# Input projection of the second and third token group by seven block products for eight (RetNet and HGRN2 decoder layer, one core)

## The chip, the cores and the metric

The kernel runs on one core of a Trainium2 chip. The metric is device time in microseconds of one execution, the median of several; lower is better. TensorE (PE) multiplies 128x128 weight blocks with up to 512 columns of activations into PSUM; VectorE (DVE), ScalarE (ACT) and GpSimd (POOL) do everything elementwise; SyncE (SP) issues the DMAs.

## The reference, cut to what matters

One decoder layer over 2048 prompt tokens and 8 sample sequences of 8 tokens (64 tokens, each sequence with a state of its own):

```
h    = rmsnorm(x) ; proj = h @ w_in                  # 1024 -> 4096: eight parts of 4 heads x 128
rq, rk, rv, rg, hq, hf, hi, hg = split(proj)
retention(rotary(rq), rotary(rk), rv), head norm, * silu(rg)         # 4 heads
f = lb + (1 - lb) * sigmoid(hf) ; HGRN2(silu(hq), 1 - f, hi, f), head norm, * silu(hg)   # 4 heads
x   += concat(o_r, o_h) @ w_out
x   += relu(rmsnorm(x) @ w_up)**2 @ w_down           # 1024 -> 4096 -> 1024
y    = rmsnorm(x) ; also the final states of both recurrences
```

## The kernel before

**Data.** Activations lie transposed, 128 features in the partitions and tokens in the columns. Every fp32 operand is cut into two parts, `hi` (rounded to the format `F32R`) and `lo` (the rest), and a product is three matmuls: hi·hi, hi·lo, lo·hi. A weight comes from DRAM as `raw`, 128x1024, 512 KB; ACT makes `hi` (line 270), DVE makes `lo` (line 284).

**Groups.** The 2112 tokens go through in three groups (`GROUPS`): 640 prompt tokens; 768 prompt tokens; the 64 sample tokens with 640 prompt tokens (704). First all three groups are mixed, one after the other (input projection, both recurrences, output projection: about 0 to 361, 361 to 781 and 781 to 1188 us), then all three go through the feed-forward layers (1188 us to the end).

**Input projection.** `proj` (line 341) makes one column block of 128 outputs: 8 row blocks x 3 products x 2 column pieces of half a group, 48 matmuls. Each head p needs six such blocks (parts 5 = f, 4 = q, 0 and 1 = rotary q and k, 7 and 3 = the two gates) and two weights for the values (`values`, line 748, 256 columns each). PSUM tiles `pj` of two banks take turns, two in all. The input is not normalised before the product: DVE multiplies the result by the factor `rs` of each token (`normed`, line 649; the values on ACT, line 758; the rotary tables on POOL, line 594). So `norm_in` of the next group (x loaded once, cut, squares added) only has to end before the first result is read.

**Order of work.** The program is written out by hand in *ticks*: every second wide matmul calls `tick`, which issues what `at` or `later` has put down for that tick. `mixer` puts the two recurrences of one head on this agenda: six levels of decays (`exponents` on POOL, lines 894 and 895; `decays` on ACT; `decayed` on DVE, lines 905 and 906), then states, outputs and gates; it needs 174 ticks in a group of 768, while a head's projection gives 192. `side` holds a second list in ticks: `plan_sums` makes the weight sums of the feed-forward layers (line 1243) beside the mixing of groups two and three.

**Weights kept.** In the first group `next_weight` (line 318) writes `hi` and `lo` of 32 of the 40 mixing weights to DRAM; the later groups read both parts back (line 253) instead of cutting them anew. The feed-forward layers already use the seven-product scheme (`product`, line 1211, `PRODUCTS`, `OCTET`): 24 matmuls of half a group each.

**Buffers.** 44 slabs of 128x768 (`sl`), 6 load tiles (`ld`), 3 + 4 tiles `raw`/`sum`, 3 + 3 tiles `hi`/`lo`.

Of the kernel before, what the change touches and what calls it, by code (L numbers as in the profile page):

```python
# [15 lines left out]
P = 128  # L16
D = 1024
KB = D // P
# [11 lines left out]
NSLAB = 44  # L30
NLD = 6
# [9 lines left out]
GROUPS = ((0, 0, 640), (0, 640, 768), (NS, 1408, 640))  # L41
# [35 lines left out]
              ("A12", "B21", True, ((0, 0),)))  # L77

# [68 lines left out]
def in_blocks():  # L147
    for p in range(H):
        if p:
            yield from ((7, p - 1), (3, p - 1))  # L150
        yield from ((5, p), (4, p), (0, p), (1, p), ("v", p))
    yield from ((7, H - 1), (3, H - 1))

# [46 lines left out]
class Kernel:  # L200
# [43 lines left out]
    def weight(self, i):  # L244
        n = len(self.stream)
        while self.w_next < min(i + 1 + self.ahead, n):
            j = self.w_next
            e = self.stream[j]
            if e[0] == "p":
# [7 lines left out]
            while self.w_load <= j or j >= W_UQ0 and self.w_load <= j + 2 and self.w_load < n:  # L257
                if self.stream[self.w_load][0] == "p":
                    break
                k, later = self.w_load, self.w_load >= self.n_sums  # L260
                other = later and k % 7 % 2
                raw = self.raws[k] = self.wp.tile([P, WT], F32, tag="sum" if other else "raw", name="raw",
                                                  bufs=4 if other else 3)
# [22 lines left out]
    def plan_stream(self):  # L286
# [6 lines left out]
        def mixing():  # L293
            self.stream += [("p" if N_MADE <= j < N_KEPT else "w", j) for j in range(W_UQ0)]
# [8 lines left out]
        mixing()  # L303
        mixing()
# [5 lines left out]

    def next_weight(self):
# [3 lines left out]
        if N_MADE <= i < N_KEPT:  # L315
# [61 lines left out]
    def build(self):  # L377
        nc, tc, I = self.nc, self.tc, self.I
        with ExitStack() as ctx:
# [15 lines left out]
            self.wts, self.second, self.kept = {}, {}, {}  # L395
# [25 lines left out]
            for ns, p0, n in GROUPS:  # L421
# [6 lines left out]
                g.segs = [list(range(first)), list(range(first, nch))]  # L428
                gs.append(g)
            nc.scalar.dma_start(vec, I["vec"])  # L430
            nc.scalar.preload_act_table_set("natural_log_exp_and_others")
            self.norm_in(gs[0], True)
# [10 lines left out]
            self.hs = cp.tile([P, KB * P], F32R, name="hs")  # L443
# [9 lines left out]
            at = [16] + [141 + 192 * (j // 2) + 85 * (j % 2) for j in range(2 * H - 1)]  # L453
            self.plan_sums(sums[:NQ], at)
            self.mix(gs[1])
            self.out_proj(gs[1], 1, lambda: self.norm_in(gs[2], pace=12))
# [78 lines left out]
    def norm_in(self, g, start=False, pace=5):  # L535
# [6 lines left out]
        def piece(kb):  # L542
            x, hi, lo = self.x_block(g, kb, start), self.getr(), self.getr()
            if start and kb == 0:
                self.ahead = 0
                self.weight(0)
# [3 lines left out]
                                           op0=ALU.mult, op1=ALU.subtract)  # L550
            if g.ns:
# [3 lines left out]
            g.h.append((hi, lo))  # L555
            if start:
                g.x.append(x)
            else:
                g.sq = self.add_square(g, g.sq, x, nc.vector)
# [52 lines left out]
        else:  # L612
            for kb in range(KB):
                self.later(pace * kb, piece, kb)
        t0 = 66 if start else pace * KB
        self.later(0 if start else t0, tables)
        if not start:
            self.later(t0 + 9, split)
        self.later(t0 + (0 if start else 20), factor)
        self.later(t0 + 24, rotary)  # L620
        self.later(t0 + 24, factor_t)

    def mix(self, g):
        nc = self.nc
        if g.ns:
            g.qm = [self.get(), self.get()]
            for q in g.qm:
                nc.gpsimd.memset(q, 0.0)
# [3 lines left out]
        for p in range(H):  # L632
            b = {}
            if prev is not None:
                self.gates(g, prev)
            self.project(g, p, b)
            end = self.mixer(g, p, b, max(self.now, end))
# [1190 lines left out]
```

## Time and profile before

| | us |
|---|---|
| median of 3 runs | 2493.01 (2492.97 to 2494.5) |
| profiled execution, first to last instruction (its span) | 2490.7 |
| median beyond that span | 2.3 |
| PE busy / DVE / ACT / POOL in the profiled execution | 2478.4 / 1868.8 / 1246.4 / 377.3 |
| bytes moved by DMA | 525.44 MB, mean 211 GB/s |

The page gives no other time for the profiled execution than its span; what lies around it is taken as the 2.3 us to the median. A busy PE is not always a PE at its best rate, since matmuls overlap in the pipeline; so rates are read from runs of matmuls without a gap, as time by count.

### The profile page before, as it was taken

To read this page: it belongs to the slowest core of one execution; us is meant where nothing else is said; L and a number is where in the kernel's file an instruction comes from. 1 tells how busy PE (TensorE), PEld (TensorE's weight loads), DVE (VectorE), ACT (ScalarE), POOL (GpSimd) and SP (SyncE) were. 2 spreads that over 40 slices of the span, in tenths; PEclk is the share of its full clock that TensorE was granted. 3 is DMA by queue.
4 is the path that set the end of the run, shared out by engine and by line. 5 is a ranking of instruction groups with operands and counts; after the bars stand their busy time and mean duration, and the time that the engine had idled before them with its cause. 6 is when DMAs were issued, how large, how long until landed. Compare 5 with 4: busy or idle time off the path is not lost.

```text
span 2490.7 us, 41430 instructions
## 1 busy us (share of the span) xinstructions
PE 2478.4 (100%) x16520; PEld 2461.9 (99%) x16520; DVE 1868.8 (75%) x2453; ACT 1246.4 (50%) x1674; POOL 377.3 (15%) x320
## 2 busy tenths in 40 slices
PE   9999999999999999999999999999999999999998
PEld 9999999999999999999999999999999999999998
DVE  7666766667685666686775899776699878778987
ACT  6665663444464444453644545444454436445544
POOL 5223304324421442340000000000000000000000
PEclk9999999999999999999999999999999999999999
DMA  7454575465566665768876866576675545867552
GB/s 265 166 185 170 203 259 178 161 229 186 184 210 236 220 219 200 266 211 270 283 213 221 280 198 213 174 239 222 203 262 177 188 151 190 288 196 247 194 189 89
DMA packets 191655, 525.44 MB, mean 211 GB/s; under 512 B 20963, under 2 KB 62563, under 8 KB 191462
## 3 DMA queue, kind: packets, MB, share of 16 engines
q1 hardware_dynamic: 191318, 522.77, 62.3%
q8 instruction: 130, 2.13, 0.4%
q14 instruction: 63, 0.52, 0.1%
q10 hardware_dynamic: 144, 0.02, 0.0%
HBM read 389.28 MB, written 132.39 MB: 209 GB/s over the span
## 4 chain that ended last, share of the span: by engine, by line
PE 98%; DVE 1%; DMA 0%; ACT 0%; issue 0%; SPq 0%; DVEq 0%
PE pj L341 29%; PE pf L1211 26%; PE pj L1211 25%; PE pjv L748 8%; PE mm L920 2%; PE mm L1108 1%; PE po L1100 1%; PE po L1102 1%; PE mm L977 1%; PE mm L512 1%; PE mm L511 1%; PE po L784 1%; PE mm L1034 1%; PE mm L850 1%; DMA lo<-w33lo 0%; DMA slab<-x 0%
## 5 line engine op out<-in xcount | busy, mean ns | idle before, releaser
L270 ACT CAST hi<-raw 128x1024 fp32r<-128x1024 f32 x392 | 411.8, 1050 | 616.6 <-PE pf L1211 258.4
L341 PE MATMUL pj<-slab,hi 128*128 128x320 f32 (+2 forms) x3072 | 661.4, 328 | 1.8 <-DVE slab L649 1.0
L1211 PE MATMUL pf<-slab,hi 128*128 128x320 f32 (+2 forms) x2768 | 657.6, 321 | 0.0
L1211 PE MATMUL pj<-slab,hi 128*128 128x352 f32 (+2 forms) x2608 | 620.6, 322 | 0.0
L284 DVE TENSOR_TENSOR lo<-raw,hi 128x1024 fp32r<-128x1024 f32 x392 | 485.6, 1239 | 113.6 <-ACT hi L270 108.1
L341 PEld LDWEIGHTS pj<-slab,hi 128*128 128x128 f32 x3072 | 508.3, 188 | 3.9 <-DVE slab L649 1.2
L1211 PEld LDWEIGHTS pf<-slab,hi 128*128 128x128 f32 x2768 | 480.1, 188 | 0.0
L1211 PEld LDWEIGHTS pj<-slab,hi 128*128 128x128 f32 x2608 | 452.9, 188 | 0.1
L1211 PE MATMUL pf<-slab,lo 128*128 128x320 f32 (+2 forms) x1384 | 444.1, 321 | 0.0
L1211 PE MATMUL pj<-slab,lo 128*128 128x352 f32 (+2 forms) x1304 | 419.1, 321 | 0.0
L341 PE MATMUL pj<-slab,lo 128*128 128x320 f32 (+2 forms) x1536 | 379.5, 327 | 0.5 <-DVE lo L284 0.4
L341 PEld LDWEIGHTS pj<-slab,lo 128*128 128x128 f32 x1536 | 263.6, 188 | 1.6 <-DVE lo L284 1.0
L1211 PEld LDWEIGHTS pf<-slab,lo 128*128 128x128 f32 x1384 | 259.6, 188 | 0.0
L1211 PEld LDWEIGHTS pj<-slab,lo 128*128 128x128 f32 x1304 | 244.6, 188 | 0.0
L748 PE MATMUL pjv<-hi,slab 128*128 128x256 f32 x1024 | 193.3, 285 | 0.0
L1302 ACT CAST slab<-slab 128x640 fp32r<-128x640 f32 (+2 forms) x192 | 145.2, 778 | 64.0 <-DVE slab L1313 51.7
L1306 DVE TENSOR_TENSOR slab<-slab 128x640 fp32r<-128x640 f32 (+2 forms) x192 | 167.0, 884 | 8.5 <-PE pj L1211 2.8
L748 PEld LDWEIGHTS pjv<-hi,slab 128*128 128x128 f32 x1024 | 162.2, 192 | 1.4
L748 PE MATMUL pjv<-lo,slab 128*128 128x256 f32 x512 | 144.8, 283 | 0.0
L899 ACT ACTIVATE slab<-slab 128x640 f32<-128x640 f32 (+2 forms) x72 | 56.3, 782 | 147.7 <-POOL slab L895 147.4
L1556 DVE TENSOR_TENSOR slab<-pf,slab 128x640 f32<-128x640 f32 (+2 forms) x88 | 77.5, 886 | 29.4 <-PE pf L1211 28.9
L748 PEld LDWEIGHTS pjv<-lo,slab 128*128 128x128 f32 x512 | 98.1, 192 | 0.0
(222 smaller groups left out, 3009.0 us busy)
## 6 DMA issues: line engine op xcount, KB each, us to landing
raw<-w SPq DMA_DIRECT2D x264, 512.0 KB, 4.3
slab<-u SPq DMA_DIRECT2D x32, 384.0 KB, 4.8
u<-ld SPq DMA_DIRECT2D x30, 384.0 KB, 4.0
slab<-u SPq DMA_DIRECT2D x32, 352.0 KB, 5.0
u<-ld SPq DMA_DIRECT2D x30, 352.0 KB, 3.9
slab<-u SPq DMA_DIRECT2D x32, 320.0 KB, 4.6
u<-ld SPq DMA_DIRECT2D x30, 320.0 KB, 4.3
ld<-x SPq DMA_DIRECT2D x16, 384.0 KB, 3.8
```

Source lines behind the costliest of these rows:

```text
L270: self.nc.scalar.copy(hi, raw)
L284: self.nc.vector.tensor_tensor(out=lo, in0=self.second.pop(j), in1=hi.bitcast(F32), op=ALU.subtract)
L341: self.nc.tensor.matmul(pj[:, i, :T2], w, a[:, c0:c1], start=j == 0 and q == 0, stop=j == n - 1 and q == 2)
L511: self.nc.tensor.matmul(ps, self.ones_r, hi, start=True, stop=False)
L512: self.nc.tensor.matmul(ps, self.ones_r, lo, start=False, stop=True)
L748: nc.tensor.matmul(pj[:, i * 256:(i + 1) * 256], a[:, s:s + C], ww, start=kb == 0 and q == 0, stop=kb == KB - 1 and q == 2)
L899: nc.scalar.activation(x["dd", w][:, a:T], x["dd", w][:, a:T], AF.Exp)
L920: nc.tensor.matmul(ps[:, j], qk[:, cols[c]], second(qk[:, cols[c]]), start=True, stop=True)
L1211: self.nc.tensor.matmul(*a, **k)
L1302: self.nc.scalar.copy(hi[:, :g.T], B[name][:, :g.T])
L1306: self.nc.vector.tensor_tensor(out=lo[:, :g.T], in0=B[name][:, :g.T], in1=hi.bitcast(F32)[:, :g.T], op=ALU.subtract)
L1556: nc.vector.tensor_tensor(out=r, in0=ps, in1=r, op=ALU.add)
```

## The change

- **Groups** become 64 sample + 512 prompt tokens (576), 768 and 768: the sample moves into the first group.
- **Pairs of blocks.** In groups two and three the blocks of one head are taken in pairs, (5, 4), (0, 1) and (7, 3). A pair is a 2x2 arrangement of blocks of the weights (row halves by the two columns of the pair) times the 2x2 blocks of the activations (row halves by token halves). `quad` forms it by seven products in place of eight: 7 x 4 x 3 = 84 matmuls of 384 columns in place of 96. Ten pairs of each group go this way; the first head's (5, 4) and (0, 1), and all values, stay as they were.
- **Weight sums.** `plan_quads` makes S1 to S4 of each pair in the first group, on the side list, one pair every 80 ticks: four half loads (256 KB), four sums of 128x512 on POOL, four casts on ACT, four `lo` parts on DVE, eight stores of 256 KB. The other three operands are stored from the weights of group one (`next_weight`). A *unit* of 512 KB holds `hi` and `lo` of one product's weights; groups two and three read seven units for each pair, up to six ahead.
- **Activation sums.** Sums need normalised input, so `norm_in` of groups two and three reads x, adds squares, forms the factor, reads x again, scales and cuts it; `plan_sides` reads x a third time and makes T1 to T4.
- **Elementwise work.** The results need no factor any more (no `normed`, no scaled tables). In all groups `1 - f` enters as a logarithm (`lk`), so that one of the two products of `decayed` goes; several slabs are reused in place.
- **Order in groups two and three.** The last head's gates come before its values; heads are stored to DRAM (`put_heads`) and read back (`get_heads`).
- **Buffers.** 49 slabs, 5 load tiles, 4 `raw` and no `sum`.

```
-GROUPS = ((0, 0, 640), (0, 640, 768), (NS, 1408, 640))
+GROUPS = ((NS, 0, 512), (0, 512, 768), (0, 1280, 768))
+QUAD = (("A11", "B11"), ("S2", "T2"), ("S3", "T3"), ("S1", "T1"), ("A12", "B21"), ("A22", "T4"), ("S4", "B22"))
...
+    def plan_quads(self, start, each):
...
+        def make(x, name, a, op, b, into):
+            order(nc.gpsimd.tensor_tensor(out=x[into], in0=x[a], in1=x[b], op=op))
...
+        def second(x, name):
+            order(nc.vector.tensor_tensor(out=x[name].bitcast(F32R), in0=x[name], in1=x["hi", name].bitcast(F32), op=ALU.subtract))
+        def keep(x, key, name):
+            unit = self.unit(key + (name,))
+            order(nc.sync.dma_start(unit[:, :n], x.pop(("hi", name)).bitcast(F32)))
+            order(nc.sync.dma_start(unit[:, n:], x.pop(name)))
...
+            self.plan_quads(110, 80)
             self.mix(gs[0])
-            self.out_proj(gs[0], 1, lambda: self.norm_in(gs[1], pace=12))
+            self.out_proj(gs[0], 1, lambda: self.norm_in(gs[1], pace=6))
...
+        def scaled(kb):
+            x, hi, lo = self.x_block(g, kb), self.getr(), self.getr()
+            nc.vector.scalar_tensor_tensor(out=x[:, :T], in0=x[:, :T], scalar=self.vec[:, V_MIX + kb:V_MIX + kb + 1],
+                                           in1=g.rs[:, :T], op0=ALU.mult, op1=ALU.mult)
+            nc.scalar.copy(hi[:, :T], x[:, :T])
...
+    def quad(self, g):
...
+        for k, (A, B) in enumerate(QUAD):
+            if k in (0, 2):
+                t = self.pj.tile([P, 2, 512], F32, tag="pj", name="pj")
+                x[k], x[k + 1] = t[:, 0, :T2], t[:, 1, :T2]
+            ps, first = x[(0, 1, 2, 3, 0, 2, 3)[k]], k < 4
+            wh, wl = self.next_weight()
...
+                for q, (w, a) in enumerate(((wh, ah), (wh, al), (wl, ah))):
+                    nc.tensor.matmul(ps, w[:, c], a, start=first and kb == q == 0, stop=kb == KB // 2 - 1 and q == 2,
+                                     skip_group_check=not first)
...
+            if k == 0:
+                nc.scalar.copy(s[:, one], ps)
+            elif k == 1:
+                add(s[:, one], ps, s[:, one])
+            elif k == 2:
+                nc.scalar.copy(s[:, two], ps)
+            elif k == 3:
+                add(s[:, two], ps, s[:, two])
+                nc.gpsimd.tensor_tensor(out=Q[:, two], in0=s[:, two], in1=s[:, one], op=ALU.add)
+            elif k == 4:
+                nc.scalar.copy(F[:, one], ps)
+            elif k == 5:
+                add(Q[:, one], ps, s[:, one])
+            else:
+                add(F[:, two], ps, s[:, one])
...
-            nc.vector.tensor_tensor(out=Q4[:, :, 0, :], in0=D4[:, :, 0, :], in1=blocks(k, w, a)[:, :, 0, :], op=ALU.mult)
...
-        at(t + 12, tt, nc.vector, _Lazy(x, "kd"), _Lazy(x, "kd"), k)
```

More of the change, by code (lines that the diff above doesn't have):

```diff
@@ L152, in in_blocks, with in_places, in_quads @@
     yield from ((7, H - 1), (3, H - 1))
+def in_places():
+    out, i = {}, 0
+    for part, p in in_blocks():
+        out[part, p] = i
+        i += 2 if part == "v" else 1
+    return out
+def in_quads():
+    for p in range(H):
+        if p:
+            yield from ((5, 4, p), (0, 1, p))
+        yield 7, 3, p
 def lay_out_weights(w_in, w_out, w_up, w_down):
@@ L611, in norm_in @@
             self.at(24 + 2 * KB, both)
[L612 to L621, printed above, removed]
+            self.later(0, tables)
+            self.later(66, factor)
+            self.later(90, rotary)
+            self.later(90, factor_t)
+            return
+        for kb in range(KB):
+            self.later(pace * kb, squares, kb)
+        t0 = pace * KB
+        self.later(t0 + 4, split)
+        self.later(t0 + 12, factor)
+        g.h = [None] * KB
+        for k in range(KB):
+            self.later(t0 + 20 + 9 * k, scaled, k)
+        self.later(t0 + 92, tables)
     def mix(self, g):
@@ L1178, in mixer @@
             t += 4
+        if g.scaled and p < H - 1:
+            at(t + 22, self.put_heads, g, p)
         if p == H - 1:
```

333 lines of the change are left out of this document (262 added, 71 removed).

## The prediction

> **What bounds the kernel now.** I read the page's busy times first, then the busy times by stage, then who held PE, then the chain of waits for PE's rate in each stage.
>
> ```profile
> PE 2478.4 (100%) x16520; PEld 2461.9 (99%) x16520; DVE 1868.8 (75%) x2453; ACT 1246.4 (50%) x1674; POOL 377.3 (15%) x320
> ```
> ```profile
> 0.00:361.00 361.00, 358.70 (x2665) 353.43 (x2666) 258.75 (x418) 229.03 (x340) 113.71 (x100) 1.00 0.57 202
> 361.00:781.00 420.00, 420.00 (x2864) 415.44 (x2863) 286.53 (x414) 195.99 (x287) 137.87 (x104) 1.00 0.56 199
> 781.00:1188.00 407.00, 406.01 (x2904) 400.76 (x2903) 273.80 (x462) 183.12 (x295) 125.69 (x116) 1.00 0.69 236
> 1188.00:2490.00 1302.00, 1293.68 (x8093) 1292.24 (x8091) 1049.70 (x1160) 638.30 (x756) 0.00 (x0) 1.00 0.64 210
> ```
> ```profile
> PE pj L341 <- DVE slab L649: 1.0, 1, 1.0
> PE pj L341 <- DVE slab L1271: 0.8, 1, 0.8
> PE pj L341 <- DVE lo L284: 0.4, 1, 0.4
> ```
> Columns of the second fence: length, then busy PE, weight loads, DVE, ACT, POOL, granted clock, DMA share, GB/s. PE has no gap in any stage: its longest waits for data in the projections are a microsecond and less. The clock is 1.00, so there is nothing to win there. The kernel ends when PE has issued its matmuls. Fewer matmuls shorten it one for one, until another resource is late.
>
> What a matmul costs, from gapless runs in the chain of waits (start, length, count):
> ```profile
> 394.31 14.03 PE pjv L748 x117
> 478.24 4.18 PE pj L341 x24
> 1399.91 7.04 PE pf L1211 x48
> 1607.94 8.32 PE pj L1211 x48
> 2265.77 7.63 PE pf L1211 x48
> ```
> Columns 256, 384, 320, 384, 352 take 119.9, 174.2, 146.7, 173.3 and 159.0 ns. From 320 to 384 columns that is 0.417 ns a column with 13.3 ns on top, and 256 columns lie on the same line (120.0). So the column count sets the rate, though every matmul loads its own weights:
> ```profile
> L341 PEld LDWEIGHTS pj<-slab,hi 128*128 128x128 f32 x3072 | 508.3, 188 | 3.9 <-DVE slab L649 1.2 <-DVE slab L1271 1.0 <-DVE slab L549 0.2
> L341 PE MATMUL pj<-slab,hi 128*128 128x320 f32 (+2 forms) x3072 | 661.4, 328 | 1.8 <-DVE slab L649 1.0 <-DVE slab L1271 0.8
> ```
> Loads equal matmuls: the two column pieces of a block share no load today. Working on one token half at a time therefore loses nothing.
>
> **The change part by part.**
>
> *Matmuls.* A pair of blocks falls from 96 to 84 matmuls of 384 columns. Ten pairs in each of two groups: 20 x 12 = 240, at 174.2 ns = 41.8 us, all of it on the path. The Trainium skill, "TensorE: Matmul & The Clock Gate", section "Back-to-back issue gap", gives N/2.4 + 2.5 ns, 162.5 ns for 384; by that the saving would be 39.0 us. The trace has 174.2 and decides.
>
> *New group sizes.* A group has 24 x 48 + 8 x 48 = 1536 projection matmuls and 16 x 7 x 24 = 2688 in the feed-forward layers. 640 to 576 takes 32 columns off each (4224 x 13.3 ns = 56.3 us), 704 to 768 adds 173.3 − 159.0 = 14.4 ns (60.7 us). On the straight line the two cancel, by the rows they add 4.4: I take 2, the middle. Chunks and sample are only exchanged between groups.
>
> *PE's floor:* 2490.7 − 41.8 + 2 = 2450.9 in the profile; with the 2.3 us by which the median exceeds the span, 2453.2. All else has to be hidden under PE; group one is the place to look, as it loses about 18 us of cover (361 less 1536 x 13.3 ns = 20.5, plus some 3 for the sample: 343) and gains the weight sums and the sample.
>
> *DVE, group one.*
> ```profile
> L905 DVE TENSOR_TENSOR slab<-slab 128x320 f32<-128x320 f32 x40 | 31.0, 774 | 6.9 <-ACT slab L899 6.9
> L842 DVE TENSOR_TENSOR ld<-ld,mm 128x512 f32<-128x512 f32 x8 | 5.5, 684 | 7.3 <-PE mm L835 5.3 <-POOL ld L841 2.0
> L823 DVE TENSOR_TENSOR slab<-slab,con 96x512 fp32r<-96x512 f32 x16 | 10.3, 681 | 0.0
> L1306 DVE TENSOR_TENSOR slab<-slab 128x768 fp32r<-128x768 f32 x64 | 59.8, 953 | 6.7 <-ACT slab L1302 2.4 <-PE pj L1211 2.2 <-PE pf L1211 2.0
> 1350.00:1500.00 150.00, 150.00 (x1025) 150.00 (x1024) 132.16 (x152) 78.32 (x96) 0.00 (x0) 1.00 0.74 245
> 300.00:340.00 40.00, 40.00 (x289) 39.99 (x289) 34.85 (x62) 27.66 (x44) 1.57 (x1) 1.00 0.71 218
> ```
> Gone: 24 products of line 905 (18.6 us), and a tenth of what follows the group's width, which I estimate at 150 of the 258.75 us (15). New: 40 `lo` parts of 128x512 at 684 ns (27.4), the sample (16 x 681 ns, two updates of 8 x 684 ns, small operations of about 17 more: 39), one more pass over x for group two (8 x 953 ns = 7.6). 258.75 + 40 = 299 of 343 us, 87%. The windows 1350:1500 (88%) and 300:340 (87%) show such shares with PE full, so this fits on average. At the end of the stage, 300:340 narrowed by 3.5 us and with 7.6 + 8 x 0.684 added would be 44 us in 40: 4 us late there, which the stage's double PSUM tiles partly absorb. Taken 4, bounds 0 and 10.
>
> *POOL, group one.* 40 sums of 128x512, between
> ```profile
> L841 POOL TENSOR_TENSOR ld<-ld,slab 128x512 f32<-128x512 f32 x8 | 8.2, 1050 | 27.2 <-PE po L784 14.4 <-DMA lo<-w19lo 6.9 <-DMA sd21S<-raw 5.9
> L894 POOL TENSOR_TENSOR slab<-slab 128x384 f32<-128x384 f32 x24 | 33.5, 1395 | 10.3 <-DVE slab L879 7.9 <-PE mm L920 2.5
> ```
> 1.05 us and 1395 x 512/384 = 1860 ns: 42 to 74 us, with about 28 for the sample, less a tenth. POOL goes from 114 to 180 or 205 of 343 us: covered. I take the row of the same width. ACT, at 229 of 361 us, gains some 40 casts and stays under 80%: nothing.
>
> *Groups two and three, elementwise.* Per group DVE loses 24 x 911 ns (line 905 at 384 columns) and 16 factors, gains 40 adds out of PSUM, 8 more scalings and T1 to T4:
> ```profile
> L905 DVE TENSOR_TENSOR slab<-slab 128x384 f32<-128x384 f32 x24 | 21.9, 911 | 8.7 <-ACT slab L899 8.7
> L649 DVE TENSOR_TENSOR slab<-pj,slab 128x768 f32<-128x768 f32 x16 | 15.3, 953 | 16.8 <-PE pj L341 16.5
> L1190 DVE TENSOR_TENSOR slab<-po,slab 128x384 f32<-128x384 f32 x32 | 17.6, 552 | 13.5 <-ACT slab L1188 13.5
> ```
> −21.9 − 15.3 + 40 x 0.552 + 7.6 + (16 x 0.953 + 16 x 0.552 = 24.1) = +17 us on 287 of now 399: 76%. Covered on average.
>
> *PSUM in a pair.* Today a result may wait for its reader while the next block runs, 48 x 174.2 ns = 8.4 us. In a pair a bank is needed again after two products, 2 x 12 x 174.2 ns = 4.2 us. DVE and ACT work in order, so a reader queued behind long operations can now hold PE. Bounds: nothing, and one long operation (line 1243, below) in each of 20 pairs, 28 us. The nearest rows are today's three waits, 2.2 us in all; I take 3.
>
> *Start of groups two and three.* The norm now has to end before the first product: 8 x 6 ticks of squares, the factor at tick 60, eight scaled blocks to tick 134, counted from the second of eight residual blocks; from there to the next group are 7 x 18 + 48 = 174 ticks. 40 ticks, at two matmuls a tick over 10 us, are left; bounds 0 and 6 us, taken 2.
>
> *DMA.* A pair's weights rise from 2 MB in 16.7 us to 3.67 MB in 14.6 us, read up to six units (12 us) ahead. New in group one: 31.5 MB for S1 to S4 (loads 10.5, stores 21.0), the sample and a second x; 5.2 MB of stores go.
> ```profile
> ld<-in SPq DMA_DIRECT2D x14, 384.0 KB, 4.4
> ld<-x SPq DMA_DIRECT2D x16, 384.0 KB, 3.8
> 360.00:370.00 10.00, 10.00 (x60) 10.00 (x60) 2.77 (x4) 3.50 (x4) 0.00 (x0) 1.00 1.02 395
> 1150.00:1250.00 100.00, 100.00 (x659) 100.00 (x659) 73.74 (x86) 55.31 (x71) 0.00 (x0) 1.00 0.80 271
> ```
> Group one's share is 0.57 x 361 = 206 us of full DMA, at 202/0.57 = 354 GB/s. The sample adds what group three has over group two, 0.69 x 407 − 0.56 x 420 = 46 us; x 9, narrower tiles −4, stores gone −15. The 31.5 MB, in rows of 2 KB, cost 89 us at 354 GB/s or 103 at 354 x 3.8/4.4 = 306 (rows of 1.5 KB against 3 KB above). Sum 331 to 345 of 343 us: full. PE needs only its weights from it, two blocks ahead, and SP issues in order: `keep` (waiting for ACT or DVE) and a load waiting for a slab stand ahead of the next weight. I take 4 us, bounds 0 and the rival below. Groups two and three gain 27 MB each: (0.56 x 420 + 27/0.354)/399 = 0.78, under the 0.80 at which 1150:1250 had PE full.
>
> **Sum:** 2450.9 + 4 (DVE) + 3 (PSUM) + 2 (starts) + 4 (DMA) = 2463.9 in the profile, 2466 as a median.
>
> **The rivals.**
>
> *DMA in group one (slower).* If 2 KB stores and loads run no better than the sample's states (2 kinds x 4 heads x 8 x 64 KB, read and written: 8.4 MB in the 46 us, 184 GB/s), the 31.5 MB need 171 us and group one 413: 70 us over, 2453 + 70 = 2523. It makes the change a loss from 39.8 us over, that is below 224 GB/s; at 200 GB/s 2509. For it: the sum is already full at the good rate. Against: 1.5 KB rows land only 16% later.
>
> *DVE and POOL exclude each other.* In group two's levels (start, length):
> ```profile
> 404.02 1.17 POOL L895 TENSOR_TENSOR slab<-slab 128x384 f32<-128x384 f32 x1
> 404.39 1.20 DVE L905 TENSOR_TENSOR slab<-slab 128x384 f32<-128x384 f32 x1
> 405.14 1.14 POOL L894 TENSOR_TENSOR slab<-slab 128x384 f32<-128x384 f32 x1
> 405.52 1.18 DVE L906 TENSOR_TENSOR slab<-slab 128x384 f32<-128x384 f32 x1
> L284 DVE TENSOR_TENSOR lo<-raw,hi x392: 1198/1225/2679, 6.2 to 2469.2; 128x1024 fp32r<-128x1024 f32 x196
> L1243 DVE TENSOR_TENSOR raw<-raw 128x1024 f32<-128x1024 f32 x64 | 90.2, 1410 | 0.3
> ```
> POOL ends at 405.19, DVE 0.41 later, POOL 0.69 after that: they alternate, and an undisturbed 1.2 us operation took up to 2.68. If all new POOL time in group one (70 to 102 us) falls on DVE's, DVE needs 369 to 401 of 343; half of it falling into DVE's pauses or beside reads of PSUM leaves 13 to 29 over: 2466 to 2482, say 2480. The Trainium skill, "SBUF — State Buffer", section "SBUF: two separate sides", states this as an exclusive lock on a shared port pair, for DVE operations with two SBUF inputs; the trace agrees by the four rows above.
>
> *PSUM turns bound,* at its upper bound: 2453 + 28 = 2481.
>
> **How the numbers follow.** A measurement tells 0.2%, 5 us, from no change: 2488 to 2498 is "same". Forecast 0.54, all faster; exclusion 0.17 (0.02 same, 0.01 slower at its upper end); PSUM 0.11 (0.01 same); DMA 0.18 (0.03 same, 0.15 slower). Faster 0.78, same 0.06, slower 0.16. The forecast's own range is 2451 (width term zero, nothing exposed) to 2477 (2453 with the bounds of DVE and the starts, 10 + 6, and twice the DMA term, 8). For 8 in 10 it has to reach over exclusion and PSUM to the foot of the DMA case: 2451 to 2500.
>
> **What would show it.** Right: line 341 loses 960 + 960 matmuls to a new line with 1680; groups two and three about 21 us shorter on equal columns; PE busy near its span. Wrong: gaps on PE before 345 us released by SP's queue or a DMA (DMA), by DVE with long line-284 operations (exclusion), PE waiting at the pair's line on ACT or DVE adds (PSUM), or a hole at the first product of group two (norm).

## The result, and the profile after

The change makes the kernel slower: 2608.76 us (median of 3 runs, 2606.21 to 2610.48) against 2493.01, a ratio of 1.0461 with a 95% interval of 1.0442 to 1.0479. The prediction was 2466, with a range of 2451 to 2500; the sign was wrong too.

First the page's busy line of the changed kernel, then its busy times by stage. Columns of the stages: length, busy PE, weight loads, DVE, ACT, POOL, granted clock, DMA share, GB/s. They are group one, two, three, and the feed-forward layers, each from its first projection matmul.

```profile
PE 2488.5 (95%) x16280; PEld 2451.7 (94%) x16280; DVE 1933.8 (74%) x2567; ACT 1335.7 (51%) x1796; POOL 490.3 (19%) x373
```
```profile
6.00:415.00 409.00, 363.03 (x2686) 346.79 (x2687) 308.04 (x502) 243.40 (x403) 197.24 (x176) 0.95 0.76 265
415.00:859.00 444.00, 411.72 (x2744) 402.22 (x2743) 297.11 (x458) 230.56 (x326) 144.83 (x93) 0.98 0.72 253
859.00:1300.00 441.00, 411.92 (x2734) 403.15 (x2733) 277.41 (x437) 218.86 (x310) 146.40 (x93) 0.97 0.69 243
1300.00:2607.00 1307.00, 1297.53 (x8097) 1295.39 (x8096) 1049.03 (x1160) 639.70 (x756) 0.00 (x0) 1.00 0.63 211
```

The feed-forward layers are nearly as they were (1307 us, 1302 before). The mixing takes 1294 us where it took 1182 (6 to 1188). Two things fill the difference. PE, which had 2 us of gaps there before, is idle for 46.0, 32.3 and 29.1 us in the three groups (length less busy), 107 us. And the granted clock, 1.00 before, is 0.95, 0.98 and 0.97. The trace has 88.7 us at half the clock in these groups, and PE at work for 71.4 of them; at half the clock PE gets through half the matmuls (rows in the last section), so about 36 us of PE's *busy* time is stretch, not work. Without it PE's work in the mixing is 1187 − 36 = 1151 us, an estimate, against 1180 before: most of the saved 42 us is really there. The pauses and the clock cost more than three times as much.

Who held PE (line waited for, us in total, times, longest):

```profile
PE mm L1241 <- DVE slab L1170: 17.4, 6, 4.1
PE pj L828 <- ACT slab L834: 13.2, 2, 6.6
PE mm L604 <- ACT slab L434: 10.5, 6, 1.8
PE pj L427 <- DVE slab L1510: 10.3, 3, 8.1
PE pj L828 <- DVE slab L816: 10.1, 4, 3.4
PE mm L1069 <- ACT slab L1066: 6.2, 5, 2.5
```

Before, no entry of the list was over 1.1 us. The regular ones stand in groups two and three: the corners of the first level (L1241, six times: three heads in each of two groups), the pair itself on readers of PSUM (L828), and the column sums of the last level (L604, six times). The waits of L427 are in group one. No wait for SP or a DMA is among the larger ones.

### The profile page after: what moved, and what is told of

It is laid out like the page before. It is cut to its first block, busy times and chain, and to the rows that moved or that the text cites. A ratio compares the mean times of both kernels' runs of the same rounds, so it can differ in the third digit from the quotient of the medians.

```text
span 2607.0 us, 41951 instructions
## 1 busy us (share of the span) xinstructions
PE 2488.5 (95%) x16280; PEld 2451.7 (94%) x16280; DVE 1933.8 (74%) x2567; ACT 1335.7 (51%) x1796; POOL 490.3 (19%) x373
## 4 chain that ended last, share of the span: by engine, by line
PE 59%; DVE 2%; POOL 2%; issue 2%; ACT 1%; DVEq 0%; POOLq 0%; ACTq 0%
PE pf L1495 25%; PE pj L1495 24%; PE pj L828 4%; PE pj L427 3%; PE pjv L1007 1%; POOL slab L1160 1%; PE mm L1184 1%; POOL slab L1159 1%; PE po L1370 0%; PE mm L1376 0%; PE po L1368 0%; POOL slab L888 0%; DVE slab L889 0%; DVE lo L312 0%; DVE slab L1143 0%
## 5 line engine op out<-in xcount | busy, mean ns | idle before, releaser
L1495 PE MATMUL pf<-slab,hi 128*128 128x384 f32 (+1 forms) x2768 | 652.7, 321 | 0.0
L1495 PE MATMUL pj<-slab,hi 128*128 128x384 f32 (+1 forms) x2608 | 618.2, 322 | 0.0
L1495 PEld LDWEIGHTS pj<-slab,hi 128*128 128x128 f32 x2608 | 454.0, 188 | 0.0
L1495 PE MATMUL pf<-slab,lo 128*128 128x384 f32 (+1 forms) x1384 | 443.6, 320 | 0.0
L1495 PE MATMUL pj<-slab,lo 128*128 128x384 f32 (+1 forms) x1304 | 419.6, 322 | 0.6 <-DVE lo L312 0.6
L427 PE MATMUL pj<-slab,hi 128*128 128x288 f32 (+1 forms) x1792 | 364.2, 319 | 15.1 <-DVE slab L1510 10.3
L828 PE MATMUL pj<-slab,unit 128*128 128x384 f32 x1680 | 348.2, 352 | 25.1 <-ACT slab L834 13.2
L828 PEld LDWEIGHTS pj<-slab,unit 128*128 128x128 f32 x1680 | 294.8, 194 | 30.0 <-ACT slab L834 15.1
L427 PEld LDWEIGHTS pj<-slab,hi 128*128 128x128 f32 x1792 | 290.8, 191 | 18.9 <-issue 9.7
L427 PE MATMUL pj<-slab,lo 128*128 128x288 f32 (+1 forms) x896 | 214.0, 319 | 1.1 <-DVE lo L312 1.1
L1588 DVE TENSOR_TENSOR slab<-slab 128x768 fp32r<-128x768 f32 (+1 forms) x192 | 166.7, 885 | 8.8 <-ACT slab L1584 4.5
L427 PEld LDWEIGHTS pj<-slab,lo 128*128 128x128 f32 x896 | 153.0, 191 | 1.9 <-DVE lo L312 1.5
```

The source lines that it names most:

```text
L427: self.nc.tensor.matmul(pj[:, i, :T2], w, a[:, c0:c1], start=j == 0 and q == 0, stop=j == n - 1 and q == 2)
L828: nc.tensor.matmul(ps, w[:, c], a, start=first and kb == q == 0, stop=kb == KB // 2 - 1 and q == 2, skip_group_check=not first)
L1495: self.nc.tensor.matmul(*a, **k)
L1588: self.nc.vector.tensor_tensor(out=lo[:, :g.T], in0=B[name][:, :g.T], in1=hi.bitcast(F32)[:, :g.T], op=ALU.subtract)
```

## The experiments

Each run stood beside the kernel before on the same chip (2492.6 to 2494.4). The stage lengths below run from the first projection matmul of one group to that of the next, read from each trace:

| kernel | us | ratio (95%) | group 1 | group 2 | group 3 |
|---|---|---|---|---|---|
| before | 2493.0 | | 354.6 | 419.7 | 407.3 |
| after | 2608.8 | 1.0461 (1.0442–1.0479) | 409.3 | 443.7 | 441.5 |
| 1 sizes only | 2509.8 | 1.0067 (1.0050–1.0084) | 355.9 | 419.7 | 418.8 |
| 2 no pairs | 2518.2 | 1.0103 (1.0088–1.0118) | 364.1 | 420.1 | 419.2 |
| 3 no weight sums | 2564.7 | 1.0287 (1.0272–1.0303) | 368.1 | 442.6 | 441.6 |
| 4 their DMAs only | 2571.7 | 1.0316 (1.0300–1.0331) | 370.8 | 446.6 | 439.5 |
| 5 rotation later | 2598.0 | 1.0422 (1.0405–1.0440) | 411.2 | 437.1 | 434.8 |
| 6 spread, corners too | 2604.9 | 1.0451 (1.0435–1.0466) | 417.5 | 439.1 | 434.6 |
| 7 sums on DVE | 2596.5 | 1.0416 (1.0401–1.0432) | 398.5 | 443.3 | 438.9 |
| 8 = 6 + 7 | 2593.5 | 1.0401 (1.0385–1.0416) | 401.8 | 441.7 | 435.6 |
| 9 no additions | 2586.9 | 1.0367 (1.0350–1.0384) | 386.3 | 447.3 | 439.4 |
| 10 no casts, remainders | 2598.4 | 1.0419 (1.0403–1.0434) | 394.0 | 448.1 | 438.1 |
| 11 no feed-forward sums | 2584.0 | 1.0361 (1.0346–1.0377) | 415.9 | 431.1 | 424.5 |
| 12 spread, corners kept | 2570.1 | 1.0307 (1.0292–1.0322) | 413.2 | 422.2 | 420.3 |
| 13 before + short pauses | 2543.4 | 1.0195 (1.0178–1.0212) | | | |
| 14 before + long pauses | 2673.2 | 1.0719 (1.0703–1.0735) | | | |
| 15 = 12 + 7 | 2561.2 | 1.0267 (1.0252–1.0282) | 397.0 | 425.4 | 420.5 |
| 16 = 12 without sums | 2526.9 | 1.0132 (1.0117–1.0147) | 367.7 | 424.4 | 420.0 |

Group one varies by some microseconds between kernels that have the same program there (409 to 418 in after and runs 5, 6, 11 and 12). Differences of a few microseconds in that column say nothing.

### Runs 1 to 4: the change taken apart

Run 1 is the kernel before with one line of the change (and a buffer for the sample tokens set up earlier, since their group now comes first):

```
-GROUPS = ((0, 0, 640), (0, 640, 768), (NS, 1408, 640))
+GROUPS = ((NS, 0, 512), (0, 512, 768), (0, 1280, 768))
```


> The kernel before with only the new group sizes: the sample and 512 tokens in group one, 768 tokens in each of the others; no pairs, no sums of weights, the input scaled by its norm after the products as before. Theory (the loss comes from the new work: sums of weights in group one, the bursts behind the pairs in groups two and three, and the clock that falls after their pauses): 2490 to 2505 us, group one about 345 us without pauses. Rival (a narrower group one with the sample no longer covers its own vector work): group one 370 us or more and 2515 us or more. For every 10 us that this run stands over 2495, 10 us of the 116 us lost belong to the sizes.

Run 2 is the changed kernel with plain blocks:

```
-                (self.gates_quad if g.scaled else self.gates)(g, prev)
-            if g.scaled and p == 0:
-                self.plan_sides(g)
-            (self.project_quads if g.scaled and p else self.project)(g, p, b)
+                self.gates(g, prev)
+            self.project(g, p, b)
...
-            self.plan_quads(110, 80)
```


> The changed kernel without its pairs: groups two and three run plain column blocks on the input that is scaled ahead; no sums of weights, no T operands, no spilling of the head outputs. Theory (pairs and their sums cause the loss): 2490 to 2510 us, that is at least 98 us under the changed kernel. Rival (the chain of the norm ahead of groups two and three, or the rewritten evacuations and logarithms that both kinds of block share, cause it): 2540 us or more, with pauses of PE at the first product of groups two and three or at the levels.

Run 3 drops `plan_quads`; run 4 puts its loads and stores back:

```
-            self.plan_quads(110, 80)
...
+                for s in {"A11": ("S1", "S2"), "A12": ("S3",), "A22": ("S4",)}[name]:
+                    self.units[key + (s,)] = unit
```


> The changed kernel without the making of S1 to S4 in group one: their loads, sums, casts and stores are left out, and the units of A11, A12 and A22 are read in their place. Theory (POOL's sums at 1.94 us each, which hold DVE up, make the pauses of group one, and the clock falls after them): group one falls from 409 to 345 to 360 us, groups two and three stay within 5 us: 2545 to 2560 us. Rival (sample and narrower group are the cause in group one): group one stays at 395 us or more, 2595 us or more.

> As the run before, but with all DMAs of the sums: the four loads of each pair, and the eight stores, of slabs as they were loaded, to units that nobody reads. Only the four sums, four casts and four remainders of each pair are left out. Theory (engines, not transfers): within 8 us of the kernel without sums, group one up to 365 us. Rival (transfers in group one, the rival that the prediction priced at 2509 to 2523): group one stays at 395 us or more and the run stands over 2590 us.

Measured: 2509.8, 2518.2, 2564.7, 2571.7. Run 1 fell between its two cases, and run 2 eight microseconds above its theory's window, far from the rival's. Their first stage tells why (run 1, then run 2, columns as above):

```profile
6.00:362.00 356.00, 345.09 (x2688) 336.20 (x2689) 263.67 (x468) 221.03 (x360) 132.31 (x139) 1.00 0.66 224
```
```profile
6.00:370.00 364.00, 348.43 (x2689) 340.08 (x2689) 257.55 (x460) 222.58 (x364) 125.19 (x137) 0.98 0.66 227
```

PE's work in group one is 345 us, as the prediction had it (343), but 11 us of pauses appear already with the sizes alone, and 15.6 in run 2. In run 1 5.3 us of them are three waits for the residual's addition between 310 and 338 us, beside the output projection; operations of the next group's norm stand ahead of it in DVE's queue. Run 3 came out 5 us above its window for the same reason: group one is at 368 us, not at 345 to 360. Its groups two and three stay at 442, as expected. Run 4 decides the DMA rival: all transfers of the sums, without the arithmetic, cost 7 us, with DMA at 0.84 in group one. Group one missed its window here too (370.8 us, up to 365 expected).

```profile
6.00:377.00 371.00, 352.75 (x2690) 343.26 (x2690) 258.95 (x461) 222.58 (x364) 127.34 (x137) 0.97 0.84 291
```

Read one after the other, the medians split the 116 us: sizes +17, what the two kinds of block share +8, pairs +46.5 (with their sums of activations, the stores of their three other operands and the stored heads), transfers of the sums +7, their arithmetic +37. Pairs should have brought −42, so their step lost 88 us, about half of it in each group (442.6 − 420.1 + 21 = 43.5).

### Runs 9 and 10: which part of the sums

```
-            order(nc.gpsimd.tensor_tensor(out=x[into], in0=x[a], in1=x[b], op=op))     # run 9
...
-            order(nc.scalar.copy(x["hi", name], x[name]))                              # run 10
-            order(nc.vector.tensor_tensor(out=x[name].bitcast(F32R), in0=x[name], in1=x["hi", name].bitcast(F32), op=ALU.subtract))
```


> The changed kernel without the 40 sums of weights on POOL in group one: what is cast, split and stored under their names are the slabs as loaded. Theory (the sums at 1.94 us each, with what they take from DVE, are most of the 38 us between the transfers alone and the changed kernel): group one falls from 409 to 375 to 388 us, the run takes 2574 to 2588 us. Rival (the 40 casts on ACT and 40 remainders on DVE, queued among the group's own work, are most of it): group one 392 us or more, 2591 us or more.

> The complement: sums on POOL, loads and stores as in the changed kernel, without the 40 casts and 40 remainders; the stores go to units that nobody reads, and the products read A11, A12 and A22 in their place. Theory: most of the loss stays, group one 392 us or more. Rival (casts and remainders): 375 to 388 us. If the two runs together regain clearly more than 38 us or clearly less, the parts act only together (queues that fill).

Group one: 386.3 and 394.0. The additions on POOL cost 23.0 us, casts and remainders 15.3; together 38.3 of the 38.5 by which group one of the changed kernel exceeds run 4. With the scatter named above so close a sum is luck; by the medians it is 21.9 + 10.3 = 32.2 of 37.1. The theory held: the additions are three fifths to two thirds, and the parts add within the scatter.

### Run 7: the additions on the other engine

```
-            order(nc.gpsimd.tensor_tensor(out=x[into], in0=x[a], in1=x[b], op=op))
+            order(nc.vector.tensor_tensor(out=x[into], in0=x[a], in1=x[b], op=op))
```


> The changed kernel with the 40 sums of group one on VectorE (DVE) instead of GpSimd (POOL); casts, remainders and DMAs stay. Theory (POOL's sums hold DVE up while both run): DVE has 27 us more of its own work and loses no time to POOL's; group one falls from 409 to 380 to 395 us, the run takes 2578 to 2596 us. Rival (DVE's total work is the limit in group one, on whichever engine the sums hold it): group one stays at 405 us or more, 2604 us or more.

Measured 2596.5, group one 398.5: 10.8 us less. The median is just above the theory's window, group one 3.5 us above its own, and both are well under the rival's. Groups of instructions from 6 to 416 us, shape, count, busy us, mean ns, idle before; first the changed kernel, then run 7 (with its stage of group one, columns as above):

```profile
L364 POOL TENSOR_TENSOR slab<-slab 128x512 f32<-128x512 f32 x40 | 61.3, 1533 | 41.1 <-DVE slab L435 27.7 <-DMA slab<-w 10.6 <-issue 1.5
L435 DVE TENSOR_TENSOR slab<-slab 128x576 fp32r<-128x576 f32 x16 | 16.8, 1053 | 5.0 <-ACT slab L434 5.0
L655 DVE SCALAR_TENSOR_TENSOR ld<-ld,vec,slab 128x768 f32<-128x768 f32 x8 | 9.4, 1179 | 0.5 <-DMA ld<-x 0.4 <-ACT slab L444 0.2
```
```profile
L364 DVE TENSOR_TENSOR slab<-slab 128x512 f32<-128x512 f32 x40 | 29.8, 745 | 1.4 <-DMA slab<-w 1.4
L435 DVE TENSOR_TENSOR slab<-slab 128x576 fp32r<-128x576 f32 x16 | 12.9, 810 | 3.6 <-ACT slab L434 3.6
L655 DVE SCALAR_TENSOR_TENSOR ld<-ld,vec,slab 128x768 f32<-128x768 f32 x8 | 7.9, 1011 | 0.0
6.00:405.00 399.00, 361.71 (x2693) 348.76 (x2693) 313.76 (x543) 244.08 (x405) 132.81 (x136) 0.96 0.79 272
```

An addition takes 1533 ns on POOL and 745 on DVE. DVE took over 29.8 us of work, yet its busy time rose by 5.7 only (308.04 to 313.76): the other 24 us had been time in which POOL held it up. The same operations of DVE became shorter, 1053 to 810 ns in line 435. The longest pause of the changed kernel shows it in one place (timeline of POOL, DVE and PE: start, length, engine):

```profile
384.48 7.78 POOL L364 TENSOR_TENSOR slab<-slab 128x512 f32<-128x512 f32 x4 [27.73 <-DVE slab L435]
385.44 1.82 DVE L435 TENSOR_TENSOR slab<-slab 128x576 fp32r<-128x576 f32 x1
387.18 2.01 DVE L655 SCALAR_TENSOR_TENSOR ld<-ld,vec,slab 128x768 f32<-128x768 f32 x1
389.12 2.02 DVE L661 TENSOR_TENSOR slab<-ld,slab 128x768 fp32r<-128x768 f32 x1
391.06 0.74 DVE L1510 TENSOR_TENSOR slab<-pj,ld 128x576 f32<-128x576 f32 x1
391.95 1.30 PE L427 MATMUL pj<-slab,hi 128*128 128x288 f32 x4 [8.14 <-DVE slab L1510]
```

Four additions run back to back, 1.94 us each; three DVE operations beside them take double their time (810, 1011 and 954 ns on average in run 7); the residual's addition, which frees PE's PSUM tile, stands behind them in DVE's queue; PE waits 8.14 us. Run 7 doesn't free that place: the waits on line 1510 come to 14.0 us there, in four pauses of up to 4.8 us.

### Runs 5, 6, 11 and 12: load or order in groups two and three

Run 5 delays the rotation of the second pair; run 6 adds three moves of the same kind; run 12 takes one of them back.

```
-        for key, r in zip(("rq", "rk"), self.quad(g)):
-            xs = self.get()
...
+        for key, r, d in zip(("rq", "rk"), self.quad(g), (9, 22)):        # runs 5, 6, 12
+            self.later(d, turned, r)
...
-        self.sigmoids(*((o[:, :T], z[:, :T]) for o, z in zip(sg, zs)))
+        self.later(6, lambda: self.sigmoids(*((o[:, :T], z[:, :T]) for o, z in zip(sg, zs))))   # 6, 12
...
+            self.values(g, p, b)                                          # 6, 12: ahead of the last gates
...
-                at(t + late + 3 * sg + (wait if w == 2 else 9 if w >= 32 else 4), level, i, sg)
+                at(t + late + 3 * sg + (wait if w == 2 else 23 if w == 64 else 17 if w == 32 else 4), level, i, sg)   # 6 only
```


> The changed kernel with the rotary copies and products of the second pair of a head, which the change issues in one piece behind the pair, begun 9 and 22 ticks later. Theory (behind each pair ACT, DVE and POOL get four blocks' evacuations at once, and the first level, queued behind them in order, comes 3 to 4 us late to PE): the 17.4 us before the first level's corners go to under 6 us, and with the clock that falls after them the run takes 2580 to 2597 us. Rival (the chain of logarithm, scan, exponents and products is by itself too long for the 39 ticks it is given): 2600 to 2612 us, the same waits.

> As the run before, and three more of the same kind in groups two and three: the two sigmoids of a pair of gates 6 ticks later, the corners of the first two levels 14 and 8 ticks later, and in the last head the values ahead of the gates. Nothing is computed in another way. Theory (bursts, not load, stop PE in groups two and three): the 17.4, 13.2 and 10.5 us of the three largest waits go to under 12 us together, the granted clock of groups two and three goes to 0.99, and the run takes 2535 to 2565 us. Rival (ACT and DVE are simply full with pairs, so the waits come back elsewhere): over 2585 us.

Run 5: 2598.0, a microsecond above the theory's window. The wait it aimed at went from 17.4 us to 3.7, as the theory said, while the wait of the pairs on DVE rose from 10.1 to 25.6. Run 6 failed: 2604.9, in the rival's range. PE waits of run 6, then of run 12:

```profile
PE mm L1244 <- DVE slab L1302: 25.2, 8, 5.1
PE pj L828 <- DVE slab L816: 11.4, 6, 2.1
PE pj L427 <- DVE slab L1513: 10.9, 4, 8.1
```
```profile
PE pj L427 <- DVE slab L1513: 13.5, 5, 8.2
PE pj L828 <- DVE slab L816: 11.9, 6, 2.1
PE mm L1244 <- DVE slab L1173: 3.4, 2, 2.7
```

In run 6 the corners wait 25.2 us, but for line 1302, the reader of the retention scores, not for their own operand: moved to ticks 53 to 63 they met the scores of ticks 46 to 50 in the ring of four PSUM tiles `mm`. Two runs separated this from load:

> The changed kernel without VectorE's 64 sums of feed-forward weights of 1.41 us in groups two and three (90 us of DVE work that the kernel before has too); loads and stores stay, and the slabs are stored as loaded. Load theory (ACT and DVE are simply full in pairs): the idle time of groups two and three falls by over a half and each takes 425 us or less; 2575 us or less. Burst theory (the order in each engine's queue behind a pair, not the load, is late): the waits before the first level and on ACT in the last head stay, each group takes 432 us or more; 2588 us or more.

> The spread version of run six with the corners of the first two levels back at their old ticks: the second pair's rotation later, the sigmoids of the gates 6 ticks later, values ahead of the last gates. In run six the corners, moved to ticks 53 and 60, met the scores of ticks 46 to 50 in the ring of four PSUM tiles. Theory (that ring gave back what the other moves won): 2572 to 2588 us, no wait of the corners on line 1302 or its like. Rival (the other two moves are worth nothing either, since what is moved meets other work): 2594 us or more.

Run 12 confirmed its theory, and came out 2 us below its window: 2570.1, 39 us under the changed kernel, with the same operations; of the 17.4, 13.2 and 10.5 us, 3.4, 1.8 and nothing are left, and the corners' wait for line 1302 is 2.6 us in place of 25.2. Run 11 landed between its windows: the DVE work of groups two and three falls by 41.5 and 42.0 us, the groups by 12.6 and 17.0. Of the same three waits 13.7, 13.2 and 10.5 us stay, as the burst theory said; what fell is the pairs' wait for DVE, from 10.1 to 3.2. Group two of run 11, then of run 12 (columns as above):

```profile
422.00:853.00 431.00, 407.61 (x2742) 399.26 (x2741) 255.60 (x426) 230.83 (x326) 124.88 (x93) 0.98 0.74 258
```
```profile
419.00:841.00 422.00, 406.68 (x2741) 397.07 (x2740) 302.36 (x458) 227.06 (x324) 142.59 (x93) 0.99 0.75 265
```

Run 12 has 302 us of DVE work and takes 422 us, run 11 has 47 less and takes 431. So the order in the queues counts for more than the load, though a lighter DVE helps too. Of the 88 us that pairs lost, run 12 regains 43 in groups two and three; 28 us of pauses and some 10 of clock are left there. One burst in the changed kernel, in the last head of group two, shows the order:

```profile
724.00 0.83 ACT L886 COPY slab<-slab 64x768 f32<-64x768 f32 x1
724.86 0.83 ACT L885 COPY slab<-slab 64x768 f32<-64x768 f32 x1
725.71 0.83 ACT L886 COPY slab<-slab 64x768 f32<-64x768 f32 x1
726.56 1.28 ACT L1137 ACT_TABLE_LOAD   x1
727.85 1.03 ACT L1137 ACTIVATE slab<-slab,lb,a 128x768 f32<-128x768 f32 x1
728.79 1.01 ACT L1138 ACTIVATE slab<-slab,a,na 128x768 f32<-128x768 f32 x1
729.71 0.56 ACT L443 ACTIVATE slab<-mm,eps 128x384 f32<-128x384 f32 x1
730.28 1.28 ACT L444 ACT_TABLE_LOAD   x1
731.58 0.52 ACT L444 ACTIVATE slab<-slab 128x384 f32<-128x384 f32 x1
732.01 0.46 ACT L834 COPY slab<-pj 128x384 f32<-128x384 f32 x1
732.52 1.33 PE L828 MATMUL pj<-slab,unit 128*128 128x384 f32 x3 [6.59 <-ACT slab L834]
```

ACT is busy for 8 us without a pause: the copies of both rotations and the logarithms, which are issued together behind the pair, then the inverse root of a head norm, and two table loads. The 0.46 us copy that would free the pair's PSUM bank stands behind them, and PE waits 6.59 us.

### Runs 8, 15 and 16: together

> Both edits together: the work of groups two and three spread out, the sums of group one on VectorE. Theory: the two stages are independent, so the gains of the two runs before add to within 8 us; 2505 to 2550 us. Rival (what group one saves is given back later): less than two thirds of the sum.

> The two edits that gained most, together: groups two and three with the later rotation, the later sigmoids and the values ahead of the last gates; the sums of group one on VectorE. Theory (independent stages): 2570 less 12 is 2558, 2550 to 2566 us; that is still over the kernel before. Rival (the two meet): 2567 us or more.

> The spread pairs without the making of S1 to S4 in group one (the units of A11, A12 and A22 are read in their place): what pairs are worth by themselves when their bursts are spread. It is to be read against the plain blocks at 2518. Theory (pairs save 21 us of matmuls a group, and what is left of the pauses and the clock takes about all of it): 2518 to 2532 us. Rival (the rest of the loss came from group one's sums running on into group two): 2505 us or less.

Run 8 (2593.5) missed its forecast, since that was made on run 6's; against the sum of what runs 6 and 7 did save (3.8 + 12.3) it has 15.3, so the two stages are independent as far as this shows. Run 15: 2561.2, as forecast. It is the best version with pairs and their sums that was run, and 2.7% slower than the kernel before. Run 16: 2526.9, in the theory's window. Spread pairs without their sums are still 8.7 us slower than plain blocks without them (run 2): the remaining pauses (49 us in the mixing, 16 in run 2) and the clock eat all 42 us of saved matmuls. No version that was run beats the kernel before.

### Runs 13 and 14: the clock

The kernel before, with some 40 artificial pauses of PE in the feed-forward layers, where POOL has nothing else to do; m is 2 in run 13 and 8 in run 14. The added products are zeros.

```
+        if self.n_since >= 200 and not k["stop"]:
+            for i in range(2):
+                order(self.nc.tensor.matmul(ps, self.ones_r, self.zd[:, :48], start=False, stop=False, skip_group_check=True))
+                for _ in range(m * (1 - i)):
+                    order(self.nc.gpsimd.tensor_copy(self.zd, self.zz))
```


> The kernel before with some 40 short pauses of PE put into its feed-forward layers, one in 200 matmuls: PE reads a small tile of zeros and adds it to a running sum, POOL, idle there, writes the zeros anew twice, and PE reads them again. I estimate 1.2 us a pause (two casts at the 568 ns that line 554 takes for 64 columns). Clock theory (only a pause of about 2 us and more lowers the clock): the time rises by the sum of the pauses that the trace shows, some 48 us, to about 2541 us, and the clock stays at 0.99 or more. Rival (the clock falls after every pause): 1.7 us more for each, 2610 us.

> The same with eight writes in a pause, an estimated 4.5 us. Clock theory: each pause is followed by 3.4 us or more at half the clock, which costs 1.7 us of matmuls more; the time rises by 1.3 to 1.5 times the sum of the pauses in the trace, to about 2493 + 180 + 70 = 2740 us. Rival (in the changed kernel the low clock came from something else, or costs nothing since the weight loads hide it): it rises by the pauses alone, about 2673 us.

Measured 2543.4, the expected number by luck (the pauses sum to 28 us, not 48), and 2673.2 where the theory had 2740. The second is the rival's number, but not by the rival's way: the pauses came out at 103 us in all, not at 180, and the time rose by 179. PE waits of run 13 and run 14, each with the stage of the feed-forward layers:

```profile
PE pj L1222 <- POOL zd L1224: 21.5, 25, 2.7
PE pf L1222 <- POOL zd L1224: 6.6, 8, 1.5
1190.00:2530.00 1340.00, 1311.06 (x8144) 1299.59 (x8143) 1046.05 (x1151) 633.69 (x746) 39.50 (x80) 1.00 0.62 202
```
```profile
PE pj L1222 <- POOL zd L1224: 71.8, 28, 4.5
PE pf L1222 <- POOL zd L1224: 30.8, 12, 4.3
1190.00:2660.00 1470.00, 1363.87 (x8156) 1351.10 (x8155) 1050.21 (x1153) 634.68 (x747) 135.04 (x320) 0.96 0.56 184
```

From run 13 to run 14 the pauses grow by 102.6 − 28.1 = 74.5 us, and the time by 129.8. The rest stands in PE's busy time: the same number of matmuls takes 52.8 us longer, at a granted clock of 0.96. The clock accounts for it: the trace of run 14 has PE at work at half the clock for 109.7 us of the stage, that of run 13 for 6.8, and half of the difference is 51.5 us. So these pauses, 2.6 us long on average, cost about 1.7 times their length. The cause is the pause: only the number of POOL's writes differs, and DVE and ACT were busy as long in both. Of the time that run 13 rises by (49 us), 28 are pauses; PE's time in the stage rises by 21 (1311 against 1290 in the kernel before, 1190 to 2480), 3 of it for the two stretches at half the clock and some 18 for the added matmuls and weight loads.

## Why the prediction was wrong

**What held.** The matmuls: line 828 has 1680, the forecast count, at the forecast rate when nothing stops it (12 in 2.08 to 2.17 us, 173 to 181 ns each):

```profile
951.98 2.11 PE pj L828 x12
959.57 2.08 PE pj L828 x12
1355.37 12.80 PE pf L1495 x96
```

PE's floor, for the most part: the work without stretch is an estimated 29 us below the kernel before in the mixing, where about 40 were forecast. The norm costs nothing that can be seen at the start of groups two and three (run 2 against run 1, 420.1 and 419.2 us against 419.7 and 418.8). For group two it is moved rather than free: it runs at the end of group one, where the prediction saw DVE 4 us late. The place was right, and so was the size for the sizes alone (5.3 us of waits there in run 1); with the sums beside it the longest pause of group one stands there. DVE in group one was forecast at 299 us busy and came to 308, hold-ups by POOL included.

**The width term** was taken as +2 with an upper bound of 4.4. Run 1 has it at 6.8, the sum of PE's busy times of its four stages (2480.24) less that of the kernel before (2473.44). Of this 1.7 us is the stretch of 3.41 us at half the clock in its group one, and 5.1 is left, close to the bound. The rate of the new width, 288 columns, was right: 96 matmuls in 12.80 us (the last row above) are 133.3 ns each, on the prediction's line.

**The step that failed** is the cover: "this fits on average", "covered", "covered on average". From DVE shares of 87% in group one and 76% in groups two and three I concluded that elementwise work would hide, and put 13 us down for everything late (4 + 3 + 2 + 4). It was 107 us of pauses and some 36 of clock. PE waits for one queue position within some 40 ticks (14 us), and a share over 400 us says nothing of that. The kernel before ran at 87% DVE without a gap from 300 to 340 us; there a block delivers one result every 24 ticks. A pair delivers two after 42, and the sigmoids or the rotation of both then enter the in-order queues at once. Run 12 shows what that is worth: the same work, most of it moved by 6 to 22 ticks only, is 39 us faster. The head has also lost its spare time: its recurrences need 174 ticks, and the projection now gives exactly 174 instead of 192. What that costs was not tested.

- *PSUM in a pair*: taken 3, upper bound 28; the waits of line 828 measure 25.1 in the changed kernel. The mechanism, a reader queued behind other work, was right, the choice was not. I took the row nearest in kind, the kernel before's three short waits, but these came from blocks with twice the time to be read. That the bound held is partly luck: it counted one long operation in each of 20 pairs, and the trace has eight waits, two of 6.6 us behind a row of ACT operations.
- *Not on the list at all*: the first level's corners (L1241, 22.0 us with all releasers) and the column sums (L604, 12.9). I had asked what the change adds, not what existing chains stand behind it in the queues of ACT and DVE.
- *DVE, group one*: taken 4, at most 10. The arithmetic of the sums, on POOL, ACT and DVE, costs 37 us.
- *POOL*: I took 1.05 us a sum, the faster of two rows; it is 1.53 on average and 1.94 back to back, so the slower row (1.86) was the better guide.
- *The clock*: "there is nothing to win there" was true, and hid that there is something to lose. The kernel before had its 1.00 because its PE had no pauses (runs 13 and 14).

**The rivals.** *DMA*, given the largest chance of a loss, was wrong: 7 us (run 4). Its work was sized about right (0.76 of 409 us is 311 us of full DMA, forecast 331 to 345), but at a share of 0.84 with reads two blocks ahead it costs no more than that. *Exclusion* of DVE and POOL was right in kind, and its 13 to 29 us are about the size of what the additions cost in group one, 23.0 us (run 9); moving them to DVE regains 10.8 of these net of their own work there (run 7). It was one cause among several, not the loss by itself. The rule of the Trainium skill, "SBUF — State Buffer", section "SBUF: two separate sides", an exclusive lock on a port pair that the two share, agrees with run 7's rows, in which DVE's other operations shorten as soon as POOL's additions go (1053 to 810 ns).

**Left open.** What makes group one vary by up to 8 us between kernels that share its program wasn't tried. Why sizes alone bring 11 us of pauses to group one was not taken further than the waits (5.5 us on line 1226, the residual's addition, in run 1). What would remove the pauses that run 12 leaves in groups two and three wasn't tried either.

## What to carry to other kernels

A busy share by stage shows that work can be hidden, not that it will be: for every result that an edit delivers in larger lots, list what enters each in-order queue at that tick and which short operation behind it frees PE. PE without pauses has two things to lose, the pause and the clock after it: to the length of a pause of about 2 us or more add the 1.7 us that 3.41 us at half the clock take away, or a multiple. For run 14's pauses that came to 1.7 times their length. When a wait is moved, look at what shares its PSUM ring before choosing the new tick.

## What the hardware showed

The granted clock answers to pauses far shorter than a stage. In each run the stretches at half the clock begin on one fixed grid of 3.413 us, and two pauses of run 13 show what decides. One of 1.89 us from 1217.79, which the grid cuts in two, left the clock at 1.00. One of 2.39 us from 1493.49, which lies within one step, was followed by a step at half, with 13 matmuls where the next has 25 (columns as above, one row a step):

```profile
1215.99:1219.40 3.41, 1.80 (x14) 1.66 (x12) 2.58 (x4) 2.26 (x3) 1.48 (x2) 1.00 0.45 154
1219.40:1222.81 3.41, 3.12 (x21) 3.12 (x22) 2.44 (x4) 0.47 (x1) 0.23 (x1) 1.00 0.73 250
1492.47:1495.88 3.41, 1.02 (x9) 0.76 (x7) 2.98 (x4) 0.86 (x2) 2.66 (x2) 1.00 0.45 138
1495.88:1499.29 3.41, 3.41 (x13) 3.41 (x14) 0.00 (x0) 0.00 (x0) 0.00 (x0) 0.50 0.24 96
1499.29:1502.71 3.42, 3.42 (x25) 3.42 (x24) 2.68 (x4) 1.68 (x2) 0.00 (x0) 1.00 0.02 5
```

The traces of all 18 kernels agree. Their 222 stretches at half the clock, the last one of each run left out, all begin on such a grid and last one to five steps. A step at full clock in which PE was idle for 1.9 us or more was followed by one at half in 177 of 178 cases; after less than 1.25 us it was so in 2 of some 12,800; between these, both happen. The Trainium skill, "TensorE: Matmul & The Clock Gate", section "HAM oscillation — how this bites in real kernels", warns of PE gaps over about 3.4 us; the runs here show that 2.4 us is enough. In the changed kernel the clock fell 2.4 us into the 8.14 us pause of group one and stayed at half for 10.24 us, three steps, 4.6 of them with PE at work.
